# Two blocks in one kernel, second block: where the norm weights are multiplied in, and how the weight matrices are split

## The chip, the cores and the metric

The kernel runs on one core of a Trainium2 chip. The metric is the device time of one execution in microseconds. A measurement of the kernel is the median of several runs.

## The reference, cut to what matters

One sequence of 256 tokens with 1024 features runs through a first block (attention and pooling mixer, then a mixture of experts) and then through a second block of two layers. The change is in the second block alone, which computes this:

```python
def rms_norm_2(x, w):
    xf = x.astype(jnp.float32)
    y = xf * lax.rsqrt(jnp.mean(xf * xf, axis=-1, keepdims=True) + RMS_EPS)
    return (y * w.astype(jnp.float32)).astype(x.dtype)

def second_block(x, ...):
    for layer in range(DEPTH_2):
        h = rms_norm_2(x, attn_norm_w[layer])
        proj = h @ w_in[layer]                      # 1024 -> 3072
        ...                                         # three mixers on the parts of proj
        x = x + mixed @ w_out[layer]                # 1024 -> 1024
        h = rms_norm_2(x, mlp_norm_w[layer])
        x = x + jnp.square(jax.nn.relu(h @ w_up[layer])) @ w_down[layer]   # 1024 -> 4096 -> 1024
    return rms_norm_2(x, final_norm_w)
```

The norm has a factor for each token (the root of the mean square) and one for each feature (w). Since h goes straight into a matmul, the token's factor can be applied to the product, and the feature's factor either to the rows of the weight matrix or to the features of x.

## The kernel before

The second block is `phase_c`, from about 668 us on. Before it comes the first block, whose experts fill TensorE; the change does not touch it. The tokens lie in two tiles of 128 (index t). `self.x` holds x token by token; `self.hT` holds x transposed, features on the partitions, in two halves of 512 features (index n), each of four blocks of 128 features.

All matmuls of the second block have fp32 precision from two rounded parts: an operand w is split into hi (w rounded, by ACT) and lo = w - hi (by VectorE), and a product takes three matmuls, hi with hi, hi with the other operand's lo, and lo with hi (`tok_step1`, lines 230 to 232; `feat_step`, lines 240 to 242). hT is split in the same way (`hT.t[0]` and `hT.t[1]`; in the trace hT00, hT01 are the hi parts of the two halves, hT10, hT11 the lo parts).

The weights come in pieces by DMA on SyncE's queue. `halves` takes such a piece of four k-steps (128 x 512 each) as two pairs of 1024 columns, and `split` makes hi and lo of a pair. For w_out and w_down that is one ACT cast (line 206) and one VectorE subtraction (line 207) of 1024 columns. For w_in and w_up it is two ACT operations and two VectorE operations of 512 columns (lines 202 and 203), since the norm weight of the feature, a column of `vcols` or `g0` with one value for each partition, is multiplied in and is another one for each k-step. The pool of the splits has four buffers for each part, so three or four splits run ahead of TensorE, and ACT waits for TensorE to give a buffer back.

`into_hT` transposes half the features of one token tile: four TensorE transposes into one PSUM tile (tp, line 294), then one ACT cast to hi (line 303) and one VectorE subtraction to lo (line 304), 128 x 512 each. It runs sixteen times: at the start of the block, between mixer and MLP and between MLP and mixer, each time twice for the first half and twice for the second. The first half is transposed behind the last parts of w_out or w_down, the second half (`late`) in the first part of the stage that follows.

A mixer layer (`mix_layer`) runs the projections z (columns 512 to 1023), q and v (0), the rotated queries and keys (1536, 2048), values (2560), and the rest (1024), then w_out. Work of the scan, of the attention and of the Fourier mixer is put between the k-steps as generators (`bg`). The rotation's two products rx and rt (lines 1605, 1606) are VectorE's, their sum (line 1607) POOL's or VectorE's; TensorE transposes it (prot, line 1617). In the attention the transposed probabilities are copied out of PSUM by ACT and VectorE in turn (pT, line 1672) for the product po (line 1680). An MLP layer (`mlp_layer`) runs eight chunks of w_up, then w_down, with the next chunk's `up` ahead of a chunk's `down`.

The order of the instructions on each engine is not the order of the code: a scheduler reorders them engine by engine by its own model of durations, and each engine runs its list strictly in order. So other operations give other lists.

## Time and profile before

| | us |
|---|---|
| median of 3 runs (lowest, highest) | 1308.5 (1306.8, 1309.25) |
| profiled execution | 1306.97 |
| its span, first to last instruction | 1305.2 |
| TensorE busy in it | 1253.0 |
| VectorE busy | 680.5 |
| ACT busy | 510.7 |
| POOL busy | 200.7 |

The mean granted TensorE clock was 0.989 of full speed. In the traces PE is TensorE, DVE VectorE, ACT ScalarE, POOL GpSimd. A row of a timeline has the start, the duration, the engine, the line of the kernel, the operation with its output and inputs, and in brackets how long the engine stood idle before and for whom it waited. Operations on one engine overlap a little, so that the next one starts before the duration of the one before is over. Matmuls are pipelined: a matmul of 512 columns is shown with 0.39 us and the next one starts 0.23 us later.

### The profile page before, as it was taken

How to read it: one execution, taken by the hardware profiler on the slowest of the kernel's cores; microseconds unless marked ns; L12 is line 12 of the kernel's file. 1: busy time of each engine (PE TensorE's matmuls, PEld its weight loads, DVE VectorE, ACT ScalarE, POOL GpSimd, SP SyncE). 2: the span in 40 equal slices, each digit the busy share in tenths (PEclk: the TensorE clock that was granted, in tenths of full speed). 3: DMA queues.
4: the chain of work that ended last, by engine and by line, in shares of the span. 5: the costliest groups of instructions: out<-in, count | busy, mean ns of one | idle time of the engine just before them, and what ended most of it. 6: DMA issues, size and time to landing. Idle time of an engine off the chain costs nothing. (4 is left out here: it accounts for less than half of the span.)

```text
span 1305.2 us, 19758 instructions
## 1 busy us (share of the span) xinstructions
PE 1253.0 (96%) x7985; PEld 875.2 (67%) x7985; DVE 680.5 (52%) x1164; ACT 510.7 (39%) x919; POOL 200.7 (15%) x270
## 2 busy tenths in 40 slices
PE   6999988999999999899999999999999999999997
PEld 3889976344443443333357678998988767989896
DVE  3698797122122221212157965655557994765654
ACT  2456433111110111101056465555556555655544
POOL 0011030000000000000024541211113461211211
PEclk9999998999999999999999999999999999999999
DMA  9998797999999999999975342655554423555550
GB/s 326 372 340 276 266 381 266 409 416 429 426 429 427 426 427 427 426 428 421 419 305 187 114 130 90 223 181 186 193 193 158 161 82 126 188 177 193 193 162 33
DMA packets 102597, 359.37 MB, mean 275 GB/s; under 512 B 8772, under 2 KB 17856, under 8 KB 87656
## 3 DMA queue, kind: packets, MB, share of 16 engines
q1 hardware_dynamic: 101832, 357.00, 72.1%
q8 instruction: 63, 1.03, 0.3%
q0 software_dynamic: 480, 1.07, 0.2%
q14 instruction: 30, 0.25, 0.1%
q10 hardware_dynamic: 192, 0.02, 0.0%
HBM read 357.00 MB, written 1.06 MB: 274 GB/s over the span
## 5 line engine op out<-in xcount | busy, mean ns | idle before, releaser
L207 DVE TENSOR_TENSOR wl<-w,wh 128x1024 fp32r<-128x1024 f32 x128 | 156.5, 1227 | 100.9 <-ACT wh L206 100.9
L206 ACT CAST wh<-w 128x1024 fp32r<-128x1024 f32 x128 | 134.1, 1050 | 144.4 <-PE up L241 65.8
L202 ACT ACTIVATE wh<-w,vcols 128x512 fp32r<-128x512 f32 x176 | 121.2, 718 | 78.9 <-PE dn L231 34.7
L203 DVE SCALAR_TENSOR_TENSOR wl<-w,vcols,wh 128x512 fp32r<-128x512 f32 x176 | 131.1, 778 | 36.5 <-ACT wh L202 34.4
L241 PE MATMUL up<-hT,wh 128*128 128x256 f32 x512 | 142.4, 278 | 0.0
L242 PE MATMUL up<-hT,wl 128*128 128x256 f32 x512 | 142.4, 279 | 0.0
L240 PE MATMUL up<-hT,wh 128*128 128x256 f32 x512 | 142.4, 278 | 0.0
L1015 PE MATMUL pu<-w,xT 128*64 128x512 f32 x512 | 121.5, 608 | 5.4 <-DMA w<-in_w_expert_up_dram 5.4
L1015 PE MATMUL pg<-w,xT 128*64 128x512 f32 x512 | 119.5, 604 | 0.0
L1101 ACT CAST yh<-y 128x512 fp32r<-128x512 f32 x32 | 19.8, 618 | 253.6 <-DVE y L1100 187.9
L1015 PE MATMUL py<-w,actT 128*64 128x512 f32 x480 | 108.0, 593 | 1.4 <-DMA w<-in_w_expert_down_dram 1.4
L231 PE MATMUL dn<-wh,actl 128*128 128x512 f32 x256 | 101.3, 396 | 0.0
L230 PE MATMUL dn<-wh,acth 128*128 128x512 f32 x256 | 101.2, 395 | 0.0
L232 PE MATMUL dn<-wl,acth 128*128 128x512 f32 x256 | 101.2, 396 | 0.0
L241 PEld LDWEIGHTS up<-hT,wh 128*128 128x128 f32 x512 | 96.9, 189 | 0.6
L240 PEld LDWEIGHTS up<-hT,wh 128*128 128x128 f32 x512 | 96.2, 188 | 0.6
L242 PEld LDWEIGHTS up<-hT,wl 128*128 128x128 f32 x512 | 96.0, 188 | 0.5 <-DVE wl L203 0.5
L1803 POOL TENSOR_TENSOR relu<-relu 128x256 f32<-128x256 f32 x64 | 53.6, 838 | 265.9 <-ACT relu L1802 265.9
L230 PE MATMUL b<-wh,hT 128*128 128x512 f32 x224 | 92.0, 412 | 2.4 <-ACT wh L202 1.9
L232 PE MATMUL b<-wl,hT 128*128 128x512 f32 x224 | 89.4, 403 | 2.3 <-DVE wl L207 1.5
L1100 DVE SCALAR_TENSOR_TENSOR y<-py,ws,gate 128x512 f32<-128x512 f32 x30 | 22.5, 751 | 128.7 <-PE py L1015 127.2
L1015 PEld LDWEIGHTS pu<-w,xT 128*64 128x64 f32 x512 | 38.0, 139 | 76.9 <-issue 67.1
(411 smaller groups left out, 2273.3 us busy)
## 6 DMA issues: line engine op xcount, KB each, us to landing
w<-in_w_expert_up_dram SPq DMA_DIRECT2D x26, 2048.0 KB, 25.7
w<-in_w_expert_down_dram SPq DMA_DIRECT2D x26, 2048.0 KB, 27.2
w<-in_w_expert_gate_dram SPq DMA_DIRECT2D x24, 2048.0 KB, 25.4
w<-in_w_in_dram SPq DMA_DIRECT2D x40, 1024.0 KB, 6.5
w<-in_w_up_dram SPq DMA_DIRECT2D x32, 1024.0 KB, 5.4
w<-in_w_down_dram SPq DMA_DIRECT2D x32, 1024.0 KB, 5.0
w<-in_w_ada_dram SPq DMA_DIRECT2D x24, 1024.0 KB, 9.8
w<-in_w_expert_gate_dram SPq DMA_DIRECT2D x16, 1024.0 KB, 10.3
```

The source lines that it names most:

```text
L202: self.nc.scalar.activation(hi[:, c], v[:, c], AF.Copy, scale=g[:, i:i + 1])
L203: self.nc.vector.scalar_tensor_tensor(lo[:, c], v[:, c], g[:, i:i + 1], hi[:, c].bitcast(F32), op0=ALU.mult, op1=ALU.subtract)
L206: self.last_hi = self.nc.scalar.copy(hi, v).ins
L207: self.last_lo = self.nc.vector.tensor_tensor(lo, v, hi, op=ALU.subtract).ins
L230: nc.tensor.matmul(ps, hT.tok(0, k, t), wh, start=first, stop=False)
L231: nc.tensor.matmul(ps, hT.tok(1, k, t), wh, start=False, stop=False)
L232: nc.tensor.matmul(ps, hT.tok(0, k, t), wl, start=False, stop=last)
L240: nc.tensor.matmul(o, hi[:, c], hT.mov(0, k), start=first and m % 2 == 0, stop=False, skip_group_check=True)
L241: nc.tensor.matmul(o, hi[:, c], hT.mov(1, k), start=False, stop=False, skip_group_check=True)
L242: nc.tensor.matmul(o, lo[:, c], hT.mov(0, k), start=False, stop=last and m % 2 == 1, skip_group_check=True)
L1015: queue["last"] = f(*args, **kw).ins
L1803: nc.gpsimd.tensor_tensor(r, r, r, op=ALU.mult)
```

## The change

`split` loses its scaled form: every pair of 1024 columns is now split by one ACT cast and one VectorE subtraction, for w_in and w_up too. The norm weight is multiplied in where x is transposed: `into_hT` gets the column of norm weights, and in place of one cast and one subtraction of 128 x 512 it runs, for each of the four blocks of 128 features, an ACT operation that scales and rounds and a VectorE operation that scales and subtracts, all of 128 x 128 and all from the one PSUM tile. Each mixer layer hands the MLP's norm weights to the transposes at its end, and the MLP of layer 0 those of the second mixer. The lines of the changed kernel are smaller by 3 to 8 (split 199 and 200, `tok_step1` 222 to 224, `feat_step` 232 to 234, transposes 286, the pieces 295 and 296).

```diff
@@ -192,17 +192,10 @@
-    def split(self, v, g=None):
+    def split(self, v):
 
         hi = self.sp.tile([128, 1024], F32R, name="wh", tag="wh")
         lo = self.sp.tile([128, 1024], F32R, name="wl", tag="wl")
-        if g is not None:
-            for i in range(2):
-                c = slice(512 * i, 512 * i + 512)
-                self.nc.scalar.activation(hi[:, c], v[:, c], AF.Copy, scale=g[:, i:i + 1])
-                self.nc.vector.scalar_tensor_tensor(lo[:, c], v[:, c], g[:, i:i + 1], hi[:, c].bitcast(F32),
-                                                    op0=ALU.mult, op1=ALU.subtract)
-            return hi, lo
         self.last_hi = self.nc.scalar.copy(hi, v).ins
         self.last_lo = self.nc.vector.tensor_tensor(lo, v, hi, op=ALU.subtract).ins
         return hi, lo
...
@@ -294,10 +286,14 @@
-    def into_hT(self, t, n):
+    def into_hT(self, g, t, n):
 
         src = self.transposed(self.x[:, t, n * 512:n * 512 + 512])
-        self.split_into(self.hT.t[0][n][:, t], self.hT.t[1][n][:, t], src)
+        for b in range(4):
+            hi, lo = (self.hT.t[i][n][:, t, b] for i in range(2))
+            c = g[:, 4 * n + b:4 * n + b + 1]
+            self.nc.scalar.activation(hi, src[:, b], AF.Copy, scale=c)
+            self.nc.vector.scalar_tensor_tensor(lo, src[:, b], c, hi.bitcast(F32), op0=ALU.mult, op1=ALU.subtract)
...
@@ -1371,7 +1367,7 @@
                     if n == 0:
-                        self.into_hT(t, n)
+                        self.into_hT(self.g0, t, n)
...
-            late = [partial(self.into_hT, t, 1) for t in range(2)]
+            late = [partial(self.into_hT, self.g0, t, 1) for t in range(2)]
...
@@ -1409,7 +1405,8 @@
             win = a["w_in_2"][layer]
-            gw = self.norm_cols("attn_norm_w_2", 1) if layer else self.g0
+
+            gw = self.norm_cols("mlp_norm_w_2", layer)
...
-                self.tok_part(ps, hT, win, 0, c0, True, False, bg, g=gw[:, 0:4])
+                self.tok_part(ps, hT, win, 0, c0, True, False, bg)
...
-                self.tok_part(ps, hT, win, 4, c0, False, True, bg, g=gw[:, 4:8])
+                self.tok_part(ps, hT, win, 4, c0, False, True, bg)
...
-                    late.append(partial(self.into_hT, t, n))
+                    late.append(partial(self.into_hT, gw, t, n))
...
-            gw = self.norm_cols("mlp_norm_w_2", layer)
             hT = self.hT
...
-                self.feat_part(ps, hT, wu, 8, 0, f * 512, g=gw[:, 0:4])
+                self.feat_part(ps, hT, wu, 8, 0, f * 512)
...
-                self.feat_part(ps, hT, wu, 8, 4, f * 512, g=gw[:, 4:8])
+                self.feat_part(ps, hT, wu, 8, 4, f * 512)
...
-                        todo.append(partial(self.into_hT, t, n))
+                        todo.append(partial(self.into_hT, self.norm_cols("attn_norm_w_2", 1), t, n))
```

The scheduler gives other orders, at three places the following ones. In the excerpts a name has its buffer's number, and the brackets hold the engines or queues whose semaphore an instruction waits for.

ACT at the start of the second block, before: z are the two evacuations of the first projection, the sums into ss are squares for the norm, wh_4826 (further up), wh_4845, wh_4864 and wh_4895 are the four splits of the next projection.

```order
L270 ACTIVATE mT10_4637,ss_4661<-xnew_4634 128x512 [waits Activation_49]
L202 ACTIVATE wh_4845<-w_4823,g0_748 128x512
L1433 ACT_TABLE_LOAD [waits PE_49]
L1433 ACTIVATE z_4812<-b_4681,rc_4755 128x512 [waits Pool_49]
L270 ACTIVATE mT10_4637,ss_4663<-xnew_4634 128x512 [waits DVE_49]
L202 ACTIVATE wh_4845<-w_4823,g0_748 128x512
L1433 ACTIVATE z_4812<-b_4682,rc_4772 128x512 [waits PE_49,Pool_49]
L202 ACTIVATE wh_4864<-w_4823,g0_748 128x512 [waits DMAHW2_49]
L202 ACTIVATE wh_4864<-w_4823,g0_748 128x512
```

The same place after; the four splits of the next projection are wh_4842, wh_4859, wh_4876 and wh_4905.

```order
L199 CAST wh_4842<-w_4839 128x1024 [waits DMAHW0_49]
L295 ACTIVATE hT01_79<-tp_4742,g0_748 128x128 [waits DVE_49]
L262 ACTIVATE mT10_4637,ss_4673<-xnew_4634 128x512 [waits Activation_49]
L199 CAST wh_4859<-w_4839 128x1024 [waits PE_49]
L1430 ACT_TABLE_LOAD [waits PE_49]
L1430 ACTIVATE z_4828<-b_4693,rc_4775 128x512 [waits Pool_49]
L262 ACTIVATE mT10_4637,ss_4675<-xnew_4634 128x512 [waits DVE_49]
L199 CAST wh_4876<-w_4839 128x1024 [waits DMAHW2_49]
L1430 ACTIVATE z_4828<-b_4694,rc_4792 128x512 [waits PE_49,Pool_49]
L199 CAST wh_4905<-w_4839 128x1024
```

The second evacuation of z stood behind two of the four splits and stands behind three.

TensorE between mixer and MLP, before: wo are the last matmuls of w_out, tp the transposes of the first half, mT the mixers' output.

```order
L230 MATMUL wo_5855<-wh_6015,mT00_4635 128x512
L231 MATMUL wo_5855<-wh_6015,mT10_4637 128x512
L294 MATMUL tp_6031<-ident_69,xnew_4634 128x128 [waits DVE_49]
L294 MATMUL tp_6031<-ident_69,xnew_4634 128x128 x3
L294 MATMUL tp_6054<-ident_69,xnew_4634 128x128 [waits DVE_49]
L294 MATMUL tp_6054<-ident_69,xnew_4634 128x128 x3
L232 MATMUL wo_5854<-wl_6016,mT00_4635 128x512 [waits DVE_49]
L232 MATMUL wo_5855<-wl_6016,mT00_4635 128x512
L230 MATMUL wo_5854<-wh_6015,mT00_4635 128x512
```

The same place after; up is the first product of the MLP.

```order
L222 MATMUL wo_5831<-wh_5991,mT00_4635 128x512
L223 MATMUL wo_5831<-wh_5991,mT10_4637 128x512
L286 MATMUL tp_6007<-ident_69,xnew_4634 128x128 [waits DVE_49]
L286 MATMUL tp_6007<-ident_69,xnew_4634 128x128 x3
L286 MATMUL tp_6036<-ident_69,xnew_4634 128x128 [waits DVE_49]
L286 MATMUL tp_6036<-ident_69,xnew_4634 128x128 x3
L232 MATMUL up_6077<-hT00_78,wh_6080 128x256 [waits Activation_49]
L224 MATMUL wo_5830<-wl_5992,mT00_4635 128x512 [waits DVE_49]
L224 MATMUL wo_5831<-wl_5992,mT00_4635 128x512
L222 MATMUL wo_5830<-wh_5991,mT00_4635 128x512
```

The first matmul of the MLP, which needs the ACT pieces of both token tiles, has been moved from behind the last w_out matmuls to ahead of those with the lo part.

VectorE at the same place, before: xnew is x with the product of w_out added, wl_6093 and wl_6123 are the first two splits of w_up.

```order
L207 TENSOR_TENSOR wl_6039<-w_4683,wh_6038 128x1024 [waits Activation_49]
L304 TENSOR_TENSOR hT10_80<-tp_6031,hT00_78 128x512 [waits Activation_49]
L304 TENSOR_TENSOR hT10_80<-tp_6054,hT00_78 128x512 [waits Activation_49]
L1766 TENSOR_TENSOR xnew_4634<-wo_5854,xnew_4634 128x512 [waits PE_49]
L1766 TENSOR_TENSOR xnew_4634<-wo_5855,xnew_4634 128x512 [waits PE_49]
L203 SCALAR_TENSOR_TENSOR wl_6093<-w_4683,vcols_82,wh_6092 128x512 [waits DMAHW7_49,DVE_49]
L203 SCALAR_TENSOR_TENSOR wl_6093<-w_4683,vcols_82,wh_6092 128x512
L203 SCALAR_TENSOR_TENSOR wl_6123<-w_4683,vcols_82,wh_6122 128x512 [waits DVE_49]
```

The same place after, where wl_6081 is the first split of w_up.

```order
L296 SCALAR_TENSOR_TENSOR hT10_80<-tp_6007,vcols_82,hT00_78 128x128 [waits Activation_49]
L200 TENSOR_TENSOR wl_6021<-w_4695,wh_6020 128x1024
L296 SCALAR_TENSOR_TENSOR hT10_80<-tp_6007,vcols_82,hT00_78 128x128 [waits Activation_49]
L296 SCALAR_TENSOR_TENSOR hT10_80<-tp_6036,vcols_82,hT00_78 128x128 [waits PE_49]
L296 SCALAR_TENSOR_TENSOR hT10_80<-tp_6007,vcols_82,hT00_78 128x128 [waits Activation_49] x2
L296 SCALAR_TENSOR_TENSOR hT10_80<-tp_6036,vcols_82,hT00_78 128x128 [waits Activation_49]
L1763 TENSOR_TENSOR xnew_4634<-wo_5830,xnew_4634 128x512 [waits PE_49]
L296 SCALAR_TENSOR_TENSOR hT10_80<-tp_6036,vcols_82,hT00_78 128x128 [waits Activation_49]
L1763 TENSOR_TENSOR xnew_4634<-wo_5831,xnew_4634 128x512 [waits PE_49]
L296 SCALAR_TENSOR_TENSOR hT10_80<-tp_6036,vcols_82,hT00_78 128x128 [waits Activation_49]
L200 TENSOR_TENSOR wl_6081<-w_4695,wh_6080 128x1024 [waits DMAHW7_49,DVE_49]
```

The additions into x, which stood next to each other, have pieces of the first half between and behind them, and the first split of w_up is one operation.

## Rows read from the trace of the kernel before

**Rows 1.** The view by stretches, core 0: columns stand in its first line

```profile
core 0: us, PE busy (x) PEld busy (x) DVE busy (x) ACT busy (x) POOL busy (x), PEclk, DMA share, GB/s
695.80:699.10 3.30, 3.30 (x10) 2.56 (x9) 3.30 (x6) 2.98 (x5) 0.00 (x0) 0.50 0.22 41
707.00:738.00 31.00, 27.91 (x393) 21.77 (x400) 30.83 (x60) 14.06 (x24) 15.02 (x16) 0.98 0.43 137
736.80:740.10 3.30, 3.30 (x62) 2.61 (x60) 2.73 (x8) 1.17 (x2) 1.44 (x3) 0.50 0.02 5
860.00:930.00 70.00, 70.00 (x447) 62.87 (x447) 39.95 (x53) 39.34 (x67) 10.47 (x13) 1.00 0.56 186
```

**Rows 2.** Groups by line and shape, 690 to 1306 us: busy, mean | idle, releaser

```profile
L203 DVE SCALAR_TENSOR_TENSOR wl<-w,vcols,wh 128x512 fp32r<-128x512 f32 x176 | 131.1, 778 | 36.5 <-ACT wh L202 34.4
L202 ACT ACTIVATE wh<-w,vcols 128x512 fp32r<-128x512 f32 x176 | 121.2, 718 | 78.9 <-PE dn L231 34.7 <-PE b L231 18.0 <-PE wo L231 8.9
...
L207 DVE TENSOR_TENSOR wl<-w,wh 128x1024 fp32r<-128x1024 f32 x80 | 97.6, 1225 | 93.5 <-ACT wh L206 93.5
...
L206 ACT CAST wh<-w 128x1024 fp32r<-128x1024 f32 x80 | 84.0, 1050 | 89.9 <-PE up L241 65.8 <-PE wo L231 14.4 <-PE dn L231 9.6
...
L304 DVE TENSOR_TENSOR hT<-tp,hT 128x512 fp32r<-128x512 f32 x12 | 7.7, 682 | 0.0
...
L303 ACT CAST hT<-tp 128x512 fp32r<-128x512 f32 x12 | 6.3, 573 | 0.0
```

**Rows 3.** Waits of TensorE, 690 to 1306 us: total, times, longest

```profile
PE prot L1617 <- POOL rx L1607: 5.8, 2, 2.9
```

**Rows 4.** TensorE's timeline at the block's start: start, us, instruction, idle before

```profile
691.62 0.50 PE L232 MATMUL b<-wl,hT 128*128 128x512 f32 x1 [0.60 <-DVE wl L203]
...
692.20 0.39 PE L231 MATMUL b<-wh,hT 128*128 128x512 f32 x1
692.43 0.40 PE L232 MATMUL b<-wl,hT 128*128 128x512 f32 x1
694.54 0.50 PE L230 MATMUL b<-wh,hT 128*128 128x512 f32 x1 [1.72 <-ACT wh L202]
```

**Rows 5.** ACT's timeline at the same place

```profile
693.20 0.69 ACT L1433 ACTIVATE z<-b,rc 128x512 f32<-128x512 f32 x1 [2.95 <-POOL rc L1241]
```

**Rows 6.** TensorE's, then VectorE's timeline before the rotation

```profile
735.66 0.44 PE L1617 MATMUL prot<-ident,rx 128*128 128x128 f32 x2 [2.90 <-POOL rx L1607]
...
732.99 0.68 DVE L1605 TENSOR_TENSOR rx<-b,cosr 128x512 f32<-128x512 f32 x1
...
735.38 0.51 DVE L1545 TENSOR_TENSOR hES<-hES,hIP 128x256 f32<-128x256 f32 x1
```

**Rows 7.** TensorE's, then VectorE's timeline at the attention's output

```profile
766.79 1.51 PE L1680 MATMUL po<-pT,cv 128*64 128x256 f32 x12 [1.00 <-DVE pT L1672]
...
764.92 1.21 DVE L207 TENSOR_TENSOR wl<-w,wh 128x1024 fp32r<-128x1024 f32 x1
```

**Rows 8.** From mixer to MLP: TensorE's, ACT's and VectorE's timeline

```profile
803.83 0.72 PE L232 MATMUL wo<-wl,mT 128*128 128x512 f32 x2
...
810.07 0.39 PE L242 MATMUL up<-hT,wl 128*128 128x256 f32 x1
...
801.78 0.72 ACT L202 ACTIVATE wh<-w,vcols 128x512 fp32r<-128x512 f32 x1 [1.44 <-PE wo L231]
...
803.64 1.05 ACT L303 CAST hT<-tp 128x512 fp32r<-128x512 f32 x2
...
809.27 2.74 DVE L203 SCALAR_TENSOR_TENSOR wl<-w,vcols,wh 128x512 fp32r<-128x512 f32 x4
```

**Rows 9.** From MLP to mixer: TensorE's timeline

```profile
984.53 0.50 PE L230 MATMUL b<-wh,hT 128*128 128x512 f32 x1 [0.47 <-ACT hT L303]
```

**Rows 10.** ACT alternating with VectorE on two PSUM tiles: ACT's timeline

```profile
779.64 0.50 ACT L1701 COPY fw<-f 128x129 f32<-128x129 f32 x2
780.32 0.46 ACT L1703 COPY fw<-f 128x127 f32<-128x127 f32 x2 [0.18 <-DVE fw L1702]
```

13 lines of the change are left out of this document (6 added, 7 removed).

## Prediction

> **What bounds the kernel now.** The view by stretches comes first. In the middle of an MLP (860 to 930 us) TensorE is busy 70.00 of 70.00 us at a granted clock of 1.00, while VectorE has 39.95 and ACT 39.34 [rows 1]. TensorE sets the time there, and the splits of the weights, which are most of what the change alters, lie beside it. In the scan of the first mixer (707 to 738) it is another picture: VectorE is busy 30.83 of 31.00 us, TensorE 27.91 [rows 1]. So the second view is what TensorE waits for from 690 us on. The list is short: 5.8 us for the rotated queries and keys (prot, two waits, one per layer) [rows 3]; then, on the timelines, 1.00 us in each layer for the attention's transposed probabilities (po) [rows 7], 0.60 and 1.72 us for splits at the block's start [rows 4] and 0.47 us at the way from MLP to mixer [rows 9]. All of it is about 11 us out of 616. The third thing to see is the clock: two short stretches, 695.8 to 699.1 and 736.8 to 740.1, have a granted clock of 0.50 (1.2 GHz in place of 2.4) [rows 1], the first right behind the stalls of 0.60 and 1.72 us [rows 4], the second right behind the 2.90 us wait of prot [rows 6]. A third like the second follows in layer 1. In 3.3 us at half clock 1.65 us of work is done, so each stretch costs about 1.65 us.
>
> **Part 1, merged splits.** A k-piece pair (1024 columns) takes two ACT operations of 718 ns and two VectorE operations of 778 ns before; a single one takes 1050 and 1225 ns, as the splits of w_out and w_down already do [rows 2]. There are 112 such pairs (224 halves; the trace shows 213 of them). ACT loses 112 x (1436 - 1050) = 43 us of busy time, VectorE 112 x (1556 - 1225) = 37 us. On the path this is worth **0** in the MLPs and most of the projections, since TensorE has no gap to give back [rows 1]. Its other side: the first half of a merged split is ready later, 1225 ns in place of 778 ns after its start, where TensorE stands waiting for it.
>
> **Part 2, the scaled pieces.** Sixteen half-transposes are taken out of PSUM. Before: one ACT cast (573 ns) and one VectorE subtraction (682 ns) [rows 2]. After: four of each at 128x128, and each ACT piece waits for VectorE's piece before it on the same tile. The trace of before has no such piece. Its nearest row is the Fourier copy, which has the same alternation on two tiles at nearly the same width: ACT takes two copies in 0.50 us, VectorE two, and ACT goes on 0.68 us after it began, 0.18 us of that spent waiting for VectorE [rows 10]. I take 0.68 us for a round of two tokens' pieces, four rounds 2.7 us; the bounds are 0.5 us (ACT's own time alone) and 1.25 us (573 + 682 ns, the whole old pair, if a piece cost as much as a half).
>
> **Where it meets the path.** Five places, each from the order of before and after and the durations above.
>
> A, *block start.* ACT has to serve the z projection's evacuations, the second of which (693.20) waits 2.95 us for a scalar from POOL [rows 5]. Whatever stands behind it in ACT's order waits too. Before, two of the next projection's four splits are ahead of it; after, three are (first excerpt of the order). One more split is 12 matmuls at 0.23 us (692.20 to 692.43), 2.7 us of cover, more than the 0.60 + 1.72 us of stall [rows 4]; with the stalls the half-clock stretch (1.65) should go: -4.0. Against that the first projection starts on pieces: four rounds of 0.68 plus a merged split of 1.05 that lies between them, 3.8 us, where two casts and two subtractions took 1.05 + 1.28 = 2.3; with the sums of squares in between I take 1.7 us. **A = -2.3**, bounds -4.0 (pieces hidden) and +1.0 (pieces at the upper price, 2.3 us more over four rounds, and clock still falling).
>
> B, *prot, both layers.* VectorE works almost without a gap from 707 to 738 us [rows 1], and the rotation's first product starts at 732.99 [rows 6]. Seven splits lie ahead of it. Back to back, four halves take 2.74 us, so a half that follows another costs 0.65 to 0.7 of its 0.778 us and a pair 1.33 [rows 8]; a merged one with the same overlap comes to 1.15: 7 x 0.18 = 1.26 us earlier. One step of the scan's products (hES, 0.51 us at 735.38 [rows 6]) is moved ahead of the rotation in the new order: 0.8 us net. **B = -1.6** for two layers; bounds 0 and -2.9 each. The clock stretch behind it I leave in, since 2.1 us of waiting stays. The Trainium skill (Perfetto Trace Analysis, Optimizing Scalar/DVE Operations) gives about 60 ns of busy overhead for a VectorE instruction on SBUF; by it a merged split saves 0.06 us, seven of them the 0.4 us of the moved step, B would be 0 and the sum 1.6 us higher. The rows' 0.18 us stands against it, from this kernel's own operations.
>
> C, *po.* VectorE's copy of the probabilities comes behind a w_out split of 1.21 us begun at 764.92, and TensorE waits 1.00 us [rows 7]. In the new order the copy is ahead of that split; ACT's copy, which ends about half a microsecond earlier, is then the last. **C = -0.9** for two layers; bounds 0 and -2.0.
>
> D, *mixer to MLP, both layers.* Before, TensorE passes with almost no gap at 803.83 and 810.07 [rows 8]. After, it has put the first MLP matmul, which needs both tokens' first ACT pieces, ahead of the last w_out matmuls (second excerpt). ACT's split at 801.78 is 1.05 in place of 0.72 us, so the sums of squares behind it and then the pieces start at 804.0 and not at 803.64 [rows 8]; two pieces more (0.50) and TensorE goes on at about 804.7: +0.9. Everything behind it on TensorE moves along. Then VectorE: before, the four halves of the first two w_up splits start at 809.27, and the first half lets TensorE go on at 810.07. After, two pieces (0.6 us) stand between the two additions into x (third excerpt), and the split is one operation, 0.46 us longer than the half: +1.1 more, TensorE at about 812.1. **D = +4.0** for two layers; bounds +0.7 each (only the merged split) and +4 each (pieces at the upper price).
>
> E, *MLP to mixer.* The wait of 0.47 us for the first cast [rows 9] becomes one for two pieces behind a longer split (+0.3), and the first merged lo split is one operation behind a piece and an addition (+0.7). **E = +1.0**, bounds 0 and +2.5.
>
> The last 0 terms: POOL and the load queue keep their order but for one pair of instructions; the first block isn't touched.
>
> Sum: -2.3 - 1.6 - 0.9 + 4.0 + 1.0 = **+0.2 us**. The profiled execution took 1306.97 (its span 1305.2 and 1.8 around it), so 1307.2 for one like it; the median of the runs (1308.5) is 1.5 above it: **1308.7 us**. About 80 us of engine work are saved, and next to none of it is where anybody waits.
>
> **The rivals.**
> *The clock comes back (faster).* If prot's waits shrink enough that the two stretches of 0.50 behind them vanish, 2 x 1.65 = 3.3 us go; with A's pieces hidden (another 1.7) the time is 1308.7 - 3.3 - 1.7 = 1303.7; with the first alone 1305.4. For it: the wait of 1.00 us at po [rows 7] is not among the places with such a stretch. Against: 2.1 us of waiting remain by B, and 0.60 + 1.72 us were enough at the start.
> *The alternation stops TensorE at the changeovers (slower).* Place: A and D, where TensorE has nothing but the pieces to wait for. It decides when a round takes 1.25 us in place of 0.68: D then loses 2 x 0.6 = 1.2 us more per layer, and its two waits come to more than 2.3 us, the sum behind which the clock fell in [rows 4], 1.65 us per layer. 1308.7 + 2.4 + 3.3 = 1314.4; without the clock 1311.1, with the clock alone 1312.0. For it: ACT's pieces stand in a queue with whole splits. Against: the row of 0.68 us. The Trainium skill (Perfetto Trace Analysis, Optimizing Scalar/DVE Operations) says that engines which aren't saturated but cause bubbles may serve sooner when their instructions are broken up; the merged split at D is the reverse of it, and no run here yet shows which way the pieces weigh.
> *Nothing reaches the path.* The waits of before stay as they are and the pieces hide: 1308.5. It can't be told from the forecast.
>
> **How the numbers follow.** Something like the sum or the third rival: 0.46. Faster by over 0.2% (2.6 us, about what a measurement of this kernel can tell from no change): 0.26, the first rival and A or B at their better bounds. Slower by over 0.2%: 0.28, the second rival and D at its upper bound. The range: 1304 where the first rival holds nearly in full, 1313.5 a little short of the second; about one in ten is left at each side.
>
> **What would show it.** A: the clock at 1.00 from 690 to 700 and no wait of 1.7 us for wh. B: prot waits of about 2.1 us. C: the po waits halved. D: new waits of about 1 us each for hT pieces and for wl just behind the transposes, in both layers. Middle of the MLPs: TensorE still without a gap, VectorE and ACT about 6% less busy. Wrong would be waits inside the projections or MLPs, a clock of 0.50 behind the mixer, or pieces well over 0.68 us a round.

## The result and the profile after

The changed kernel takes **1315.9 us** (median of 7 runs, 1312.45 to 1319.6), the kernel before beside it 1309.25 (7 runs): a ratio of **1.0056, 95% interval 1.0037 to 1.0074**. It is slower by about 7 us, outside the range forecast. A second set of runs of it gave 1.0047 (1.0026 to 1.0068); the mean of the two, 1.0051, is 6.7 us. All ratios here and below are taken over fast runs, and one execution of e6, of 2485.7 us, is left out of its ratio. The profiled execution took 1319.6 us.

Its first block, which the change doesn't touch, happens to be 4.4 us longer in that execution than in the one shown of before. So the second block is counted here from ACT's first copy into x (671.39 us before, 675.80 after), and whole times are compared by medians alone. Before's profiled execution lies 1.5 us under its median of 1308.5, so the last times of the table can be that much too high. Each number is a start (the last one the end) counted in this way, minus the same of before, in us:

| landmark | forecast | after | its repeat |
|---|---|---|---|
| TensorE's transposes of z, 699.65 (before 699.32) | -2.3 | -4.1 | -4.3 |
| VectorE's entry into the scan, 703.98 (699.95) | -2.3 | -0.4 | -0.6 |
| transposes of the rotated keys, 738.17 [rows 6] | -3.1 | -1.9 | -2.1 |
| the Fourier product | -3.6 | +0.1 | +1.1 |
| first w_down matmul, layer 0 | -1.6 | +3.1 | +4.1 |
| transposes of z, layer 1 | -0.6 | +4.3 | +5.3 |
| Fourier product, layer 1 | -1.8 | +5.1 | +5.1 |
| end | +0.2 | +8.2 | +7.3 |

The view by stretches of the kernel after (columns as in [rows 1]): the scan, the half-clock stretch behind it, and the middle of an MLP.

```profile
707.00:738.00 31.00, 27.14 (x365) 21.32 (x363) 31.00 (x53) 11.63 (x15) 17.49 (x18) 1.00 0.50 162
738.10:744.80 6.70, 6.63 (x83) 4.81 (x84) 5.92 (x11) 1.17 (x2) 2.91 (x6) 0.50 0.49 151
860.00:930.00 70.00, 70.00 (x452) 63.18 (x451) 38.61 (x38) 34.58 (x52) 12.06 (x13) 1.00 0.60 194
```

VectorE is busy 31.00 of 31.00 us in the scan, and the stretch at 1.2 GHz is 6.7 us long where [rows 1] has 3.3. The MLP runs as before, ACT 12% less busy and VectorE 3%. TensorE's waits from 672 us on, after (total, times, longest):

```profile
PE prot L1614 <- POOL rx L1604: 6.6, 2, 4.0
PE up L234 <- DVE wl L200: 2.3, 2, 1.1
PE up L232 <- ACT hT L295: 1.8, 2, 0.9
PE b L224 <- DVE wl L200: 1.2, 3, 0.5
PE po L1677 <- ACT pT L1669: 0.8, 2, 0.4
PE b L222 <- ACT hT L295: 0.6, 1, 0.6
```

The first answers to [rows 3], and has grown from 5.8 us. The two waits of up weren't there before; po's have shrunk from 1.00 us each [rows 7].

**VectorE's entry into the scan.** POOL's, ACT's, VectorE's and TensorE's timeline after (start, us, instruction, idle before and for whom):

```profile
695.38 1.95 POOL L1234 TENSOR_SCALAR ssr<-ss,rs 128x2 f32<-128x2 f32 x1
698.69 0.19 POOL L1237 TENSOR_TENSOR rc<-rs 128x1 f32<-128x1 f32 x1
...
698.91 0.69 ACT L1430 ACTIVATE z<-b,rc 128x512 f32<-128x512 f32 x1 [3.19 <-POOL rc L1237]
699.50 3.88 ACT L199 CAST wh<-w 128x1024 fp32r<-128x1024 f32 x4
...
700.57 3.49 DVE L200 TENSOR_TENSOR wl<-w,wh 128x1024 fp32r<-128x1024 f32 x3 [3.38 <-ACT wh L199]
703.98 1.28 DVE L1459 COPY hIP<-pz 128x512 f32<-128x512 f32 x2
...
699.65 1.03 PE L1443 MATMUL pz<-ident,z 128*128 128x128 f32 x8
```

ACT has the third split ahead of the second evacuation, as forecast, and TensorE transposes z 4.1 us earlier. But ACT still stands 3.19 us for POOL's scalar, which comes 22.9 us after the block's start (before 21.6), its casts stand behind that, and VectorE stands 3.38 us for the first of them. Its three splits then end about where its eight halves ended before, 28.3 and 28.5 us after the block's start. The same two places of VectorE before:

```profile
694.53 5.39 DVE L203 SCALAR_TENSOR_TENSOR wl<-w,g,wh 128x512 fp32r<-128x512 f32 x8 [2.96 <-ACT wh L202]
699.95 1.29 DVE L1462 COPY hIP<-pz 128x512 f32<-128x512 f32 x2
```

There VectorE took z's transposes up 0.6 us after TensorE had begun them, after it is 4.3 us. At the scan's other end (VectorE's, then TensorE's timeline after):

```profile
735.50 0.68 DVE L1602 TENSOR_TENSOR rx<-b,cosr 128x512 f32<-128x512 f32 x1
...
738.17 0.69 PE L1614 MATMUL prot<-ident,rx 128*128 128x128 f32 x2 [4.03 <-POOL rx L1604]
```

**Mixer to MLP**, TensorE's, ACT's and VectorE's timeline after:

```profile
809.12 0.38 PE L232 MATMUL up<-hT,wh 128*128 128x256 f32 x1 [0.92 <-ACT hT L295]
...
816.80 0.38 PE L234 MATMUL up<-hT,wl 128*128 128x256 f32 x1 [1.14 <-DVE wl L200]
...
808.47 0.60 ACT L295 ACTIVATE hT<-tp,vcols 128x128 fp32r<-128x128 f32 x2
809.24 0.37 ACT L295 ACTIVATE hT<-tp,vcols 128x128 fp32r<-128x128 f32 x1 [0.17 <-DVE hT L296]
810.63 0.37 ACT L295 ACTIVATE hT<-tp,vcols 128x128 fp32r<-128x128 f32 x1 [1.02 <-DVE hT L296]
...
815.53 2.35 DVE L200 TENSOR_TENSOR wl<-w,wh 128x1024 fp32r<-128x1024 f32 x2
```

Both waits stand where term D put them. The alternating pieces cost ACT 0.17 to 1.02 us of waiting a round, the longest while VectorE's piece stands behind a whole split of 1.22 us.

### The profile page after: what moved, and what is told of

It is laid out like the page before. It is cut to its first block, busy times and chain, and to the rows that moved or that the text cites. A ratio compares the mean times of both kernels' runs of the same rounds, so it can differ in the third digit from the quotient of the medians.

```text
span 1317.8 us, 19633 instructions
## 1 busy us (share of the span) xinstructions
PE 1258.9 (96%) x7985; PEld 881.6 (67%) x7985; DVE 678.7 (52%) x1100; ACT 487.8 (37%) x855; POOL 217.1 (16%) x270
## 5 line engine op out<-in xcount | busy, mean ns | idle before, releaser
L200 DVE TENSOR_TENSOR wl<-w,wh 128x1024 fp32r<-128x1024 f32 x240 | 295.1, 1232 | 158.6 <-ACT wh L199 158.5
L199 ACT CAST wh<-w 128x1024 fp32r<-128x1024 f32 x240 | 251.1, 1050 | 275.1 <-PE dn L223 71.3
L1011 PE MATMUL pu<-w,xT 128*64 128x512 f32 x512 | 118.5, 596 | 5.4 <-DMA w<-in_w_expert_up_dram 5.4
L1799 POOL TENSOR_TENSOR relu<-relu 128x256 f32<-128x256 f32 x64 | 60.7, 949 | 254.6 <-ACT relu L1798 254.6
L222 PE MATMUL b<-wh,hT 128*128 128x512 f32 x224 | 91.7, 411 | 0.6 <-ACT hT L295 0.6
L223 PE MATMUL b<-wh,hT 128*128 128x512 f32 x224 | 88.7, 397 | 0.1
L270 POOL TENSOR_SCALAR ms<-ss 128x1 f32<-128x1 f32 x12 | 3.9, 322 | 504.1 <-DMA gf<-in_norm_f_g_dram 457.7
```

Source lines behind the costliest of these rows:

```text
L199: self.last_hi = self.nc.scalar.copy(hi, v).ins
L200: self.last_lo = self.nc.vector.tensor_tensor(lo, v, hi, op=ALU.subtract).ins
L222: nc.tensor.matmul(ps, hT.tok(0, k, t), wh, start=first, stop=False)
L223: nc.tensor.matmul(ps, hT.tok(1, k, t), wh, start=False, stop=False)
L1011: queue["last"] = f(*args, **kw).ins
L1799: nc.gpsimd.tensor_tensor(r, r, r, op=ALU.mult)
```

## The experiments

Two suspects: the pieces with the merged splits at the changeovers (D), and VectorE's queue in the scan (B). All edits are to the changed kernel unless said otherwise; only their main lines are shown. Landmarks as in the table above, in this order: transposes of z / VectorE's entry / keys / Fourier product / w_down / z of layer 1 / Fourier product of layer 1 / end.

| kernel | ratio (95%) | landmarks against before |
|---|---|---|
| e1 | 1.0012 (0.9998, 1.0026) | -4.4 / -0.8 / -2.2 / +1.0 / +2.3 / +3.1 / +3.9 / +5.2 |
| e2 | 1.0008 (0.9994, 1.0022) | -0.9 / -0.6 / -0.8 / -0.5 / +0.2 / +0.6 / +1.6 / +2.3 |
| e13 | 1.0037 (1.0022, 1.0052) | -4.1 / -0.5 / -1.9 / +0.2 / +1.5 / +2.1 / +3.9 / +6.2 |
| e8 | 0.9992 (0.9978, 1.0007) | -4.2 / -1.6 / -5.2 / -5.0 / -2.8 / -1.6 / -3.4 / -1.2 |
| e12 | 0.9981 (0.9968, 0.9993) | -0.1 / -0.1 / -1.4 / -1.9 / -1.8 / -1.8 / -3.4 / -3.5 |
| e15 | 1.0076 (1.0047, 1.0104) | -4.6 / -4.4 / -5.0 / -3.2 / +0.2 / +3.8 / +5.7 / +11.5 |
| e16 | 1.0011 (0.9994, 1.0029) | -4.6 / -4.6 / -4.6 / -4.5 / -3.2 / -0.9 / -0.7 / +2.9 |
| e17 | 1.0045 (1.0028, 1.0063) | -2.6 / -2.4 / -3.0 / -1.0 / +1.3 / +2.4 / +3.0 / +5.2 |

### e1 and e2: each part alone

e1 keeps the merged splits and takes hT back to one cast and one subtraction (the norm weights are left out).

```diff
-        for b in range(4):
...
+        self.split_into(self.hT.t[0][n][:, t], self.hT.t[1][n][:, t], src)
```

> The changed kernel with the plain half-transposes of before: one cast and one subtraction of 128x512, no scaled pieces, so the norm weights are left out of the second block. Every split stays a single operation of 1024 columns. Theory 1 (the alternating pieces cost the time at the changeovers, mixer to MLP twice and MLP to mixer once, some 5.5 us of new waits): those waits fall to those of before plus at most 0.5 us each, and the time comes to 1308 to 1311. Theory 2 (the merged splits cost it, since their first half is ready later): the waits for wl stay at about 1 us each and the time stays near 1316.

e2 keeps the pieces and splits w_in and w_up in halves of 512 again, scaled by a column of ones.

```diff
-            hi, lo = self.split(v[:, 2 * hh:2 * hh + 2, :].rearrange("p k f -> p (k f)"))
+            hi, lo = self.split(v[:, 2 * hh:2 * hh + 2, :].rearrange("p k f -> p (k f)"), two)
```

> The changed kernel with its scaled pieces, but every w_in and w_up pair split by two ACT and two VectorE operations of 512 columns as before (scaled by a column of ones, so the result is the same). Theory 1 (pieces): as slow as the changed kernel or slower, 1315 to 1319, with the first MLP matmul still ahead of the last w_out matmuls and 1 us of waiting for hT pieces there. Theory 2 (merged splits): back to about 1309.

Both medians are level with before, so neither part alone makes the 6.7 us. The landmarks say more: from z's transposes to the Fourier product e1 loses 5.4 us, as after does (4.2, repeat 5.4), and e2 0.4. That loss belongs to the merged splits, and so does the gain of 4.4 us ahead of it; what is left of both at the Fourier product is +1.0 us in e1, +0.1 in after and +1.1 in its repeat. From there to w_down after loses 3.1 and its repeat 3.0, e1 1.3, e2 0.8: a third of it takes both parts together. (0.8 us of it in after, the repeat and e1, and none in e2, is the spacing of up's matmuls, on which more below.) e1's waits:

```profile
PE prot L1610 <- POOL rx L1600: 6.6, 2, 4.0
PE b L222 <- ACT hT L295: 1.3, 2, 0.8
PE up L234 <- DVE wl L200: 0.9, 2, 0.5
```

The waits of up come to 0.9 us in e1, 1.2 in e2, 4.1 in after.

### r_after: the changed kernel again

> The changed kernel once more, unaltered, for a second profile: which of its parts repeat. Expected to repeat: the waits at the changeovers (0.9 and 1.1 us per layer) and the prot waits within 0.2 us. Expected to differ by some us: when the second block starts, and how long the stretch at half clock behind prot is. Time 1314 to 1318.

1.0047, landmarks as in the first table: the loss and its places are no accident of one execution.

### e3, e4, e6 and e13: other ways through the changeovers

e3 records ACT's four pieces first and VectorE's four behind them.

```diff
+        for b in range(4):
+            self.nc.scalar.activation(self.hT.t[0][n][:, t, b], src[:, b], AF.Copy, scale=cs[b])
         for b in range(4):
```

> The changed kernel with the same pieces, but written as four ACT pieces first and then four VectorE pieces, so that an ACT piece no longer waits for VectorE's piece before it on the same tile. Theory 1 in its narrow form (it is the alternation, not the number of operations): the waits at the changeovers shrink to 1 us in all, 1309 to 1312. If the number of pieces costs it: near 1316. Theory 2 (merged splits): near 1316.

1.0040 (1.0022, 1.0058). The waits of up fall to 0.9 us, but at the block's start a new wait of 1.7 us (b for VectorE's hT) takes half of A's gain: z's transposes come 2.3 us earlier, not 4.1.

e4 multiplies the weights onto the whole PSUM tile in one VectorE operation, and then casts and subtracts.

```diff
+        self.nc.vector.tensor_tensor(xg, src, g[:, 4 * n:4 * n + 4].unsqueeze(2).to_broadcast([128, 4, 128]), op=ALU.mult)
+        self.nc.scalar.copy(hi, xg)
+        self.nc.vector.tensor_tensor(lo, xg, hi.bitcast(F32), op=ALU.subtract)
```

> The changed kernel with the norm weights multiplied onto the transposed tile by one VectorE operation of 128x512 in PSUM (weights broadcast along the tokens), then one cast and one subtraction as before. Three operations in series, about 0.7 + 0.6 + 0.7 = 2.0 us. Theory 1 (alternation): no MLP matmul ahead of w_out's last ones, waits at the changeovers under 1 us each, 1309 to 1312. Theory 2 (merged splits): near 1316.

1.0053 (1.0033, 1.0072), no better: the waits for the pieces go, but VectorE has an operation more and up waits 2.8 us for wl.

e6 splits the first four k-steps of z and of the first w_up chunk in halves.

```diff
+                self.tok_part(ps, hT, win, 0, c0, True, False, bg, two=c0 == 512)
...
+                self.feat_part(ps, hT, wu, 8, 0, f * 512, two=f == 0)
```

> The changed kernel with the scaled pieces and merged splits, except that the first four k-steps behind each set of transposes (first projection, first chunk of w_up) are split in two ACT and two VectorE operations of 512 columns. Theory 1b (at the changeovers it is the two together: pieces stand ahead of a lo split that is a single operation): the waits for wl fall from 1.1 us each to about 0.4 or less, those for hT from 0.9 to 0.6; 1311 to 1314. If each alone sets it: no change, 1316.

1.0033 (1.0008, 1.0058). The waits of up fall to 2.5 us, but z's transposes are back to -0.4 us: the merged splits of the first projection are what made A.

e13 keeps the alternation at the block's start and takes e3's order at the changeovers.

```diff
+        for bs in ([0, 1, 2, 3],) if g is not self.g0 else ([0], [1], [2], [3]):
```

> The changed kernel with four ACT pieces and then four VectorE pieces between mixer and MLP and between MLP and mixer, and the alternating pieces of the change at the block's start. Theory 1: the first MLP matmul is no longer ahead of w_out's last ones, the waits for hT there (1.8 us) go, those for wl fall from 2.3 to 0.9 us, and the start keeps its gain of 4 us (which the run with the new order everywhere lost half of): 3 to 4 us below the changed kernel, 1311 to 1313. If the changeovers do not matter: 1315 to 1317.

The waits of up fall from 4.1 to 0.9 us, A keeps its -4.1, and Fourier product to w_down costs 1.3 us as in e1, not 3.1. So the alternation at the changeovers costs 1.7 us in that layer; the ratio falls by 0.0014, 1.9 us in all, which the intervals alone don't tell from nothing. The scan is as it was.

### e5, e7 and e14: VectorE's subtractions to POOL

e5 gives POOL the lo part of four splits a layer in the rotation's projections; e7 is e5 with e3's order; e14 is e13 with two in the values' projection.

```diff
-        self.last_lo = self.nc.vector.tensor_tensor(lo, v, hi, op=ALU.subtract).ins
+        self.last_lo = (self.nc.gpsimd if pool else self.nc.vector).tensor_tensor(lo, v, hi, op=ALU.subtract).ins
```

> The changed kernel with every second lo part of the splits of the rotated queries and keys (columns 1536 to 2559 of w_in, four of 1024 columns per layer) made by POOL in place of VectorE. Theory 3 (in the scan VectorE sets the time: the 4 us that merged splits win at the block's start come back as a longer wait for the rotation, 4.0 us in place of 2.9, and a longer stretch at half clock): VectorE has 4 x 1.2 us less before the rotation's products, the prot wait falls below 1 us and the half-clock stretch behind it goes; 1308 to 1311 where the changed kernel has 1316. If the loss lies at the changeovers alone: the prot wait shrinks but the time stays within 2 us of the changed kernel's.

> Both remedies: pieces written as four ACT operations, then four VectorE operations, and the four lo parts per layer on POOL. If theory 1 (alternation at the changeovers) and theory 3 (VectorE in the scan) both hold, their gains add: 1303 to 1308, at or below the kernel before. If POOL's slow operations hold up its own part of the scan: 1312 or more.

> The run before it with two lo parts per layer on POOL, those of the value projection that lie between the two rotations on VectorE, where POOL has no rotation waiting. Theories 1 and 3 together: the second prot wait of layer 0 falls from 4.0 to about 2.6 us and the half-clock stretch is no longer than in the kernel before; 1307 to 1310, level with the kernel before or a little under it. If POOL's 2.5 us operations hold up the sum of the keys' rotation: prot's waits 4 us or more, 1313 or more.

1.0068, 1.0038 and 1.0091: a miss in all three. POOL takes 2.50 us (e5) and 2.98 (e14) for what VectorE does in 1.23. In e5 the sum of the queries' rotation stands behind such an operation on POOL, and prot waits 2.8 us there. In e14 POOL stands 2.23 us for VectorE when it comes to the sum: VectorE's own split beside POOL's two took 3.42 us, and so its rotation comes late. POOL's, VectorE's, then TensorE's timeline of e14:

```profile
726.43 5.92 POOL L200 TENSOR_TENSOR wl<-w,wh 128x1024 fp32r<-128x1024 f32 x2
...
726.67 3.42 DVE L200 TENSOR_TENSOR wl<-w,wh 128x1024 fp32r<-128x1024 f32 x1
...
738.87 1.27 POOL L1606 TENSOR_TENSOR rx<-rx,rt 128x512 f32<-128x512 f32 x1 [2.23 <-DVE rt L1605]
...
740.20 0.69 PE L1616 MATMUL prot<-ident,rx 128*128 128x128 f32 x2 [7.47 <-POOL rx L1606]
```

### e9, e10 and e11: the keys' transposes one step later

e9 is the kernel before, e10 the changed one, e11 e3, each with the keys' transposes behind the next piece of the scan and the attention one step later.

```diff
-            proj(2048, evac_rot(kT, bgs, 0))
-            att = attention()
+            proj(2048, evac_rot(kT, bgs, 1))
...
+            att = later(attention())
```

> The kernel before with the rotated keys' transposes put one step (two k-steps, 2.7 us of matmuls) into the next projection, and the attention one step later. Theory 3: the prot wait of 2.9 us per layer and the half-clock stretch behind it go, up to 4.5 us per layer; if the attention's chain is not the next thing that ends last: 1300 to 1305. If it is: its later start shows as waits at pt and po, 1306 to 1310.

> The changed kernel with the same step. Theory 3 (the gain of 4 us at the block's start is real and is given back at the rotation): prot's waits of 4.0 and 2.6 us and the half-clock stretches go, the gain at the start is kept, and the time falls by 5 to 9 us from the changed kernel's 1316, to 1307 to 1311; the difference to the same step in the kernel before is then the changeovers alone, 4 to 6 us. If the clock stretches come anyway: 1312 or more.

> The changed kernel with the pieces written as four ACT operations and then four VectorE operations, and with the step. If theories 1 and 3 hold, the changeovers' waits and the rotation's both go: 1302 to 1306, below the kernel before. If the step brings waits at the attention: 1308 to 1312.

1.0033, 1.0039 and 1.0018. At 1313.6 us e9 missed both branches of its expectation; e10 and e11, at 1314.2 and 1311.6, came out in the slower one, e10 with a half-clock stretch of 6.8 us in each layer. prot's wait is gone in e9 and down to 1.0 us in all in e10 and e11, and TensorE waits in the attention in its place. TensorE's timeline of e9, then of e10:

```profile
759.81 1.00 PE L1671 MATMUL pt<-ident,s 128*128 128x128 f32 x4 [1.51 <-POOL s L1660]
```

```profile
755.38 2.07 PE L1640 MATMUL sc<-kT,qT 64*128 64x256 f32 x6 [3.37 <-DVE s L1645]
```

In e10 VectorE works without a gap up to the product that TensorE waits for, so the wait is for VectorE's backlog and not for the rotation. In e9 it is the attention's own chain: POOL stands there 2.42 us for VectorE, and VectorE 1.05 us for ACT.

### e8 and e12: fewer subtractions in the rotation's projections

Four lo parts a layer are left out and hi is used in their place, in the changed kernel (e8) and in the kernel before (e12).

```diff
         self.last_hi = self.nc.scalar.copy(hi, v).ins
+        if pool:
+            return hi, hi
```

> The changed kernel without four of the lo parts per layer (every second split of w_in's columns 1536 to 2559): TensorE multiplies by hi a second time in their place, so it does the same number of matmuls, and the result is not the reference's. VectorE has four operations of 1.2 us less per scan and POOL none more. Theory 3 (VectorE's backlog at the rotation gives back what merged splits win at the block's start): the product rx follows the projection's end at once, prot waits about 2.5 us per layer (rx 0.6, rt 0.6, POOL's sum 1.3) in place of 4.0 and 2.6, and the time falls by 2 to 5 us from the changed kernel's, to 1311 to 1314. If VectorE does not set it: prot's waits stay and the time is within 1.5 us of the changed kernel's.

> The kernel before without the same lo parts as in the run of the changed kernel that left four out per layer (every second split of w_in's columns 1536 to 2559, here eight half operations; TensorE multiplies by hi again, so the result is not the reference's). A control for theory 3. If VectorE's backlog at the rotation is what the changed kernel pays for, the kernel before, where rx already follows the projection's end within 0.4 us, wins little: its prot waits stay near 2.5 us and its time falls by at most 3 us, to 1306 or more, against 8 us in the changed kernel. If the relief is worth the same to both, 1300 to 1302, theory 3 explains nothing of the difference between them.

The same work of VectorE is worth 0.0059 of the time in the changed kernel (1.0051 to 0.9992, 7.7 us) and 0.0019 before (2.5 us): some 5 us more, give or take 3 by the intervals. In e8 prot's wait is 0.9 us and the scan has no half-clock stretch (its view by stretches, PEclk 1.00):

```profile
725.00:755.00 30.00, 28.98 (x384) 21.64 (x383) 29.30 (x51) 14.85 (x30) 18.37 (x24) 1.00 0.34 107
```

So with VectorE relieved the change costs 1.4 us (0.9992 against 0.9981) in place of 6.7. By the landmarks it is A's gain that comes through: e8 stands at -5.0 us at the Fourier product, where after stands at +0.1, while the waits of up stay (4.2 us in e8, 4.1 in after). It is no full account: e1, whose scan loses as much as after's, is only 1.6 us above before. In e12 prot's waits fell to 1.5 us each, where 2.5 were expected.

### e15, e16 and e17: what holds VectorE's entry

z's scalar is the product of two norm scalars, made one after the other on POOL. e15 (the changed kernel) and e16 (the kernel before) leave the second out and use the first twice; e17 computes both, but makes z's scalar from the first and ahead of the second.

```diff
-            s = self.small.tile([128, 2], F32, name="ssr", tag="ssr", bufs=2)
-            nc.gpsimd.tensor_scalar(s, ssb[t], ra, ra, op0=ALU.mult, op1=ALU.mult)
-            rb = self.rsqrt(s, 2)
+            rb = ra
```

> The changed kernel without the second of the two chained norm scalars at the block's start (POOL's ssr, two ms and one rs for each token tile are left out and the first scalar is used twice, so the values differ from the reference; all other work stays). Question: why does VectorE enter the first scan only 0.4 us earlier (28.2 us after the block's start, before 28.6) although TensorE's transposes of z come 4.1 us earlier? Theory A, the chain POOL scalar -> ACT's second evacuation of z -> ACT's casts behind it -> VectorE's splits holds VectorE: the second scalar, now at 22.9 us after the block's start, comes 2.5 to 3.5 us earlier, VectorE's entry comes 1.5 to 3 us earlier, and the keys' rotation as much (60.8 to 59.4 us after the block's start in place of 62.4), with a wait of prot of 1 to 2.5 us in place of 4.0; the whole time falls by 2 to 4 us, to a ratio of 1.002 to 1.0035. Theory B, VectorE's own amount of work up to the scan sets its entry: entry and rotation stay within 0.5 us and the ratio stays at 1.0045 to 1.0055.

> The control: the kernel before with the same scalars left out (values differ from the reference for the same reason). Theory A: before, VectorE enters the scan 0.6 us behind TensorE's transposes of z, so the scalar chain and TensorE's own stalls for splits (0.60 and 1.72 us) go together; an earlier scalar gives ACT back earlier, at most the 2.3 us of stalls and the half-clock stretch behind them (1.7 us) go: entry 0.5 to 3 us earlier, ratio 0.997 to 0.9995. Theory B: nothing moves by more than 0.5 us, ratio 0.999 to 1.001. Between the two controls: if the scalar chain is a cost that the change alone lays bare, the changed kernel gains more by this edit than the kernel before does; if it gains the same or less, the chain was there already and explains no difference.

> The two kernels with one norm scalar showed that the chain through POOL's scalar holds VectorE's entry into the scan (entry 24.2 us after the block's start in place of 28.2, keys' rotation 59.3 in place of 62.4, prot's wait 2.6 in place of 4.0 us), and yet they weren't faster: in both, the up matmuls of the MLPs follow each other at 119.9 ns in all chunks, where they take 113.5 and 117.8 in turn in every other run (768 x 2 x 3.6 to 4.7 ns, 5.6 to 7.2 us in all). In both, a small tile was gone and the buffers of the splits stood 64 bytes lower in SBUF. This kernel keeps every tile and every operation of the changed kernel and their addresses of the splits; only the scalar for z is made from the first norm scalar alone (its square), ahead of the second, which is still computed and used by nobody (values differ from the reference for that reason). Theory A (the chain holds VectorE, the 64 bytes made the slow matmuls): up spacing back at 113.5 and 117.8, entry 24 to 25 us, keys' rotation 59 to 60, the Fourier product 2.5 to 3.5 us earlier than in the changed kernel, ratio 1.0015 to 1.0035. Rival (removing the scalars' operations, or the earlier scalar itself, costs in the MLPs): spacing stays at 119.9 and the ratio at 1.006 to 1.0085.

The chain does hold VectorE: against after, its entry comes 4.0 us earlier in e15 and 2.0 in e17, the keys 3.1 and 1.1, and prot waits 2.5 us each time in place of 4.0. VectorE's, then TensorE's timeline of e17, whose block starts at 669.40:

```profile
695.54 1.28 DVE L1459 COPY hIP<-pz 128x512 f32<-128x512 f32 x2
...
730.67 0.69 PE L1614 MATMUL prot<-ident,rx 128*128 128x128 f32 x2 [2.51 <-POOL rx L1604]
```

But it isn't new. In e16 the entry comes 4.6 us earlier too, and z's transposes come at the same time as in e15: with the scalar early, nothing is left of A's gain. What was expected of the times missed: e15 is at 1.0076, not 1.002 to 1.0035, and e17 at 1.0045, 0.8 us better than the mean of after, not 2 to 4; its entry (26.1 us), its keys (61.3) and its Fourier product (1.0 us earlier than after's) come short as well.

e15 and e16 lose their gain in the MLPs, where up's matmuls are slow. TensorE's group in e15, e17 and before (672 or 810 us on):

```profile
L234 PE MATMUL up<-hT,wl 128*128 128x256 f32 x512 | 144.7, 283 | 2.3 <-DVE wl L200 2.3
```

```profile
L234 PE MATMUL up<-hT,wl 128*128 128x256 f32 x512 | 142.2, 278 | 2.3 <-DVE wl L200 2.3
```

```profile
L242 PE MATMUL up<-hT,wl 128*128 128x256 f32 x512 | 142.4, 279 | 0.0
```

From start to start it is 119.9 ns in e15 and e16, against 113.5 and 117.8 in turn from chunk to chunk elsewhere, the first two chunks alike (in the mean 116.3 after, 115.2 before): 5.6 us over the 1536 matmuls against after, 7.2 against before. Leaving out POOL's operations had also taken a small tile away, and by the expectation of e17 the split buffers lay 64 bytes lower in SBUF (no trace shows addresses); e17, with every tile in place, has the old spacing. Whether the place of the buffers does it isn't shown: e17 has the operations back as well.

## Why the prediction was wrong, step by step

**A, the block's start: right in kind, larger in size.** The third split stands ahead of the second evacuation, the wait of 1.72 us and the half-clock stretch of [rows 1] are gone: -4.1 us, the good bound of the term. e6 shows that it is the merged split, and e16 that it is a matter of the scalar: with an earlier one before has the gain too.

**B, the rotation: the step that failed.** The forecast let A's gain run on to the rotation and took off 0.8 us for the splits. The splits' size was right: eight halves took 5.39 us, 1.35 a pair, three merged ones 3.49, 1.16 each, so 0.18 saved (forecast 0.18), and VectorE's way from its entry to the keys' rotation is 1.5 us shorter, more than 0.8. (The estimate of 0.06 us from the Trainium skill, Perfetto Trace Analysis, Optimizing Scalar/DVE Operations, which gives about 60 ns of overhead for a VectorE instruction on SBUF, is not borne out.) What was missed is where VectorE starts. [rows 5] has the row, ACT's wait of 2.95 us for POOL's scalar, and the prediction used it for TensorE's cover alone. VectorE's splits hang on ACT's casts behind that wait, so it enters the scan 0.4 us earlier and not 4.1. Part of TensorE's gain turns into a wait: 4.03 us in place of 2.90 [rows 6], where 2.1 was forecast. In layer 1, which has no such lead, the wait does fall, if less than forecast, from 2.90 us to 2.57. At the first Fourier product the forecast is 3.7 us off, in the repeat 4.7, of 8.0 and 7.1 at the end.

**The clock stretch "left in" was mis-sized.** In layer 0 it is 6.7 us in after and 10.1 in the repeat (last group of rows), against 3.3 before [rows 1]. TensorE works 6.6 and 9.2 us of it, and half of that is lost, so 1.7 and 3.0 us more than before. With C's 0.4 this makes about the +2.0 and +3.2 us from the keys to the Fourier product, where the forecast had -0.45. That the longer wait makes the longer stretch isn't shown: e2 waits as long as before and has one of 6.8 us. TensorE's timeline of e2, then its view by stretches:

```profile
735.85 0.69 PE L1623 MATMUL prot<-ident,rx 128*128 128x128 f32 x2 [2.86 <-POOL rx L1613]
```

```profile
735.20:742.00 6.80, 6.16 (x82) 4.42 (x83) 5.74 (x13) 1.17 (x2) 3.51 (x6) 0.50 0.06 5
```

**C, po: the wait fell as forecast (1.00 to 0.4 us a layer), the time didn't.** VectorE's copy did come ahead of the split, but ACT's second copy stands behind a cast. TensorE's, then ACT's timeline of layer 1 after:

```profile
1086.63 1.51 PE L1677 MATMUL po<-pT,cv 128*64 128x256 f32 x10 [0.39 <-ACT pT L1669]
...
1085.05 1.04 ACT L199 CAST wh<-w 128x1024 fp32r<-128x1024 f32 x1
1086.00 0.58 ACT L1669 COPY pT<-pt 128x512 f32<-128x512 f32 x1
```

so the first group of this product, from its first matmul to its last, takes 3.6 us in both layers, before 3.2.

**D, mixer to MLP: right in place, mechanism and waits.** Forecast 0.9 and 1.1 us a layer, measured 0.92 and 1.14. The stage as a whole costs 3.1 and 3.0 us (repeat 3.0 and 2.2), since up's two spacings come in the other order where it costs 3: the 192 matmuls ahead of the first w_down follow each other at 117.8 ns in place of 113.4, 0.8 us a layer. The rule of the Trainium skill (Perfetto Trace Analysis, Optimizing Scalar/DVE Operations) that breaking instructions up may serve sooner where engines aren't saturated but cause bubbles, holds for the splits in e6 (waits of up 2.5 us in place of 4.1). For the pieces the runs show another thing: e13 has as many of them and waits of 0.9 us, as e1 with whole operations has, so it is the alternation that costs there.

**E, MLP to mixer: right.** From layer 0's first w_down matmul to layer 1's transposes of z it costs 1.2 us, forecast 1.0.

**"Next to none of the saved work is where anybody waits": VectorE saved none.** In the second block it is busy 412.75 us before and 411.36 after; ACT saved 23 us, so of the 80 forecast some 25 were saved. VectorE's splits took 268.0 us and take 236.5, the pieces add 10, and 20 more went into operations that the change doesn't touch. The merged splits bring these 20: e1 has them as after does, e2 hardly any. VectorE's groups before, after, and the first of them in e2:

```profile
L310 DVE TENSOR_TENSOR actl<-relu,acth 128x256 fp32r<-128x256 f32 x64 | 35.2, 551 | 14.3 <-ACT acth L309 14.3
L1509 DVE TENSOR_TENSOR qt<-hq,hIP 128x256 f32<-128x256 f32 x32 | 14.2, 470 | 1.0 <-ACT hq L1466 1.0
L1545 DVE TENSOR_TENSOR hES<-hES,hIP 128x256 f32<-128x256 f32 x28 | 14.0, 518 | 0.0
```

```profile
L306 DVE TENSOR_TENSOR actl<-relu,acth 128x256 fp32r<-128x256 f32 x64 | 45.2, 706 | 3.4 <-ACT acth L305 3.4
L1506 DVE TENSOR_TENSOR qt<-hq,hIP 128x256 f32<-128x256 f32 x32 | 20.9, 693 | 0.0
L1542 DVE TENSOR_TENSOR hES<-hES,hIP 128x256 f32<-128x256 f32 x28 | 17.3, 639 | 1.4 <-POOL kt L1510 1.4
```

```profile
L313 DVE TENSOR_TENSOR actl<-relu,acth 128x256 fp32r<-128x256 f32 x64 | 35.3, 551 | 14.4 <-ACT acth L312 14.4
```

**The rivals.** The slower one came true in its sign (1314.4 forecast, 1315.9), but not by its mechanism: ACT's pieces come further apart than 0.68 us (0.77 and 1.39 from 808.47 to 809.24 and 810.63), but the two waits it wanted to grow are those of the forecast, no half-clock stretch follows them, and about half of what the forecast missed (in the repeat two thirds) lies ahead of the first Fourier product. The faster one needed shorter waits of prot, and the first grew; the third, with no change, is outside the interval.

**What stays open.** Profiles and medians don't agree on e1: its second block is 5.2 us longer than before's, its median 1.0 to 1.6 us, 3.4 at the most by the interval, and e13, with landmarks within 1 us of it, is 3 us above it. Some 1.5 us of the 5.2 can be before's profiled execution and 1.7 is the order of up's spacings in its two layers; single profiles carry that much. Why this order flips isn't settled: after and its repeat, one program, differ in it in layer 1. Nor is what sets the length of a half-clock stretch.

## What to carry to other kernels

Before a gain on TensorE is carried on through a stage, look for the engine that fills that stage and ask what *its* start hangs on; an in-order queue (here ACT behind one scalar of POOL) passes nothing on, and much of the gain returns as a wait. Merge operations where nobody waits, keep them short where one stands in front of a chain, and don't alternate two engines on one tile at a changeover (at the block's start, by e3, the alternation was the better order). Where an experiment leaves an operation out, look whether the loops that it shouldn't touch keep their pace.

## What the runs showed of the hardware that was not expected

VectorE's operations on two operands in SBUF and POOL's slow each other. POOL's timeline after, an operation alone and one beside VectorE; then VectorE's, beside POOL and alone:

```profile
883.60 0.61 POOL L1799 TENSOR_TENSOR relu<-relu 128x256 f32<-128x256 f32 x1 [14.11 <-ACT relu L1798]
885.45 1.06 POOL L1799 TENSOR_TENSOR relu<-relu 128x256 f32<-128x256 f32 x1 [1.23 <-ACT relu L1798]
...
885.95 0.83 DVE L306 TENSOR_TENSOR actl<-relu,acth 128x256 fp32r<-128x256 f32 x1
...
894.24 0.42 DVE L306 TENSOR_TENSOR actl<-relu,acth 128x256 fp32r<-128x256 f32 x1
```

44 of the 64 such VectorE operations take the longer time after and in e1, 20 before and in e2, so it comes with the merged splits. In the rows shown POOL's longer operation starts beside a split that ends at 886.04, and VectorE's longer one stands behind that split. Not every overlap does it: 15 of the 32 qt operations after stay at 0.43 us though POOL works beside them for 0.32 us in the mean. POOL's 128x2 operation (ssr) took 0.41 us in the first token tile and 1.95 beside a scaling of x and a split in the second. VectorE's operations that read PSUM don't show it (rx takes 0.68 us beside POOL, the pieces 0.34 with POOL and without). The Trainium skill (Perfetto Trace Analysis, Optimizing Scalar/DVE Operations) says that the two share an SBUF read port; the trace agrees.

The half-clock stretch that comes with one and the same wait of 4.0 us was 6.7 us in after and 10.1 in the repeat; with e14's 7.5 us it was 13.4, the last 4.4 us of the wait among them. Waits of 2.9 us had 3.3 us before and 6.8 in e2. The repeat's, then e14's stretch:

```profile
730.90:741.00 10.10, 9.22 (x89) 6.79 (x90) 9.32 (x16) 1.17 (x2) 3.78 (x7) 0.50 0.33 105
```

```profile
735.60:749.00 13.40, 8.80 (x88) 6.46 (x89) 11.63 (x21) 1.17 (x2) 6.05 (x9) 0.51 0.24 79
```
